# A decoder block's MLP, from one woven loop to two sweeps of seven products

## The chip, the cores and the metric

The kernel runs on one core of a Trainium2 chip. Its time is the device time of one execution in microseconds (us); lower is better. The five engines of a core are named as in the profile: PE multiplies matrices, DVE (VectorE) and ACT (ScalarE) work on tiles elementwise, POOL (GpSimd) and SP (SyncE) here mostly issue DMAs. PEld is PE's loading of the stationary operand, which overlaps its matmuls.

## The reference

One decoder layer on 512 tokens of width 2048, all float32. After a norm, an input projection, a delta-rule group, an attention group and an output projection, the part that the change touches is the MLP:

```python
h = h + jnp.einsum("bse,ed->bsd", mix, w_o[l])
u = rms_norm(h, mlp_norm[l])
hid = jnp.square(jax.nn.relu(jnp.einsum("bsd,df->bsf", u, w_up[l])))   # 2048 -> 8192
h = h + jnp.einsum("bsf,fd->bsd", hid, w_down[l])                      # 8192 -> 2048
return rms_norm(h, final_norm)
```

## The kernel before

**Products.** Every float32 operand is split into two float32r halves, `hi` (a rounding copy, on ACT, L147) and `lo` (the rest, a subtraction on DVE, L149). A product is then three matmuls: hi by hi, hi by lo, lo by hi. Weights come in as raw tiles of 512 KB ([128, 1024]) by DMAs of SP's queue, and `split`/`parts` makes `hi` and `lo` of each; there are 3 buffers for each of the two and 6 raw ones (`BUFS`).

**The MLP** starts at L947. `to_feature_major` scales `h`, turns it (transposes on PE, L185) and makes 16 pairs of halves `uT`, one for each 128 features. The hidden units are taken in 16 blocks of 512. `up_first` computes the first block's hidden units, 192 matmuls of 512 columns (L978 to 980). For each later block, `up_steps` computes four chunks of 128 hidden units by `cols_steps` (L204 to 206): the stationary operand is a 128x128 piece of `w_up`, the moving one all 512 tokens, so 16 feature blocks by 3 matmuls for a chunk, 192 for a block. The squared relu is L965 and L966.

**Down** goes by seven products. The block's hidden units (512 tokens by 512 units) are cut into four quarters a11 to a22 and the piece of `w_down` (512 by 1024, for each of two passes p) into four quarters b11 to b22. `seven_steps` makes seven factors of the hidden units, each split by `two` into halves that stay in SBUF (L800, L801). `block_steps` forms four sums of weight quarters on DVE (L864, 870, 878, 884) and runs seven products of 12 matmuls with 512 columns (L835 to 837), so 84 for a pass and 168 for a block, where the plain way would need 192. After most products its PSUM banks are added to `h` in SBUF, 16 additions of 128x512 a pass (L850, 852).

**Order.** The code's order is each engine's order. The loop at L996 weaves: while block b goes down, one step of the down products stands between pieces of the up product of blocks b+1 and b+2, and of the factors of block b+1. Block 15 goes down without the seven products (L1020 to 1036), woven with the end of block 14, and the final norm and the stores of the output follow by token tiles. SP issues a raw tile's load as soon as one of the 6 buffers is free.

Of the kernel before, what the change touches and what calls it, by code (L numbers as in the profile page):

```python
# [12 lines left out]
F32 = mybir.dt.float32  # L13
F32R = mybir.dt.float32r
AF = mybir.ActivationFunctionType
# [16 lines left out]
def hybrid_block(ctx: ExitStack, tc: tile.TileContext, x, attn_norm, w_in, conv_w, a_log, dt_bias,  # L32
# [758 lines left out]
    weave(chain(attn_values(1, dv[1]), attn_cols(2, df[2]), attn_cols(3, df[3])), att)  # L791


    def half_tile():

        return big("p", [P, 2, 2, 256], nm="hf")

    def two(src):
        z = big("w", [P, 2, 2, 256], F32R, nm="op")
# [4 lines left out]
    def seven_steps(left, f):  # L804

        a11, a21, a12, a22 = left[0][:, 0], left[0][:, 1], left[1][:, 0], left[1][:, 1]
        f["a12"] = two(a12)
        yield
        f["a11"] = two(a11)
        z = big("m", [P, 2, 2, 256], nm="s12")  # L810
        s1, s2 = z[:, 0], z[:, 1]
        V.tensor_add(s1, a21, a22)
        yield
        f["s1"] = two(s1)
        V.tensor_sub(s2, s1, a11)
        yield
        f["s2"] = two(s2)
        s4 = s1
        V.tensor_sub(s4, a12, s2)
        yield  # L820
        f["s4"] = two(s4)
        s3 = s2
        V.tensor_sub(s3, a11, a21)
        yield
        f["s3"] = two(s3)
        yield
        f["a22"] = two(a22)
        yield

    def product(bank, fac, wts, first, last_):  # L830
        (ah, al), (bh, bl) = fac, wts
        for k in range(2):
            for t in range(2):
                st = slice(t * P, (t + 1) * P)
                T.matmul(bank[t], lhsT=ah[:, k, st], rhs=bh[:, k, :], start=first and k == 0, stop=False, skip_group_check=True)  # L835
                T.matmul(bank[t], lhsT=ah[:, k, st], rhs=bl[:, k, :], start=False, stop=False, skip_group_check=True)  # L836
                T.matmul(bank[t], lhsT=al[:, k, st], rhs=bh[:, k, :], start=False, stop=last_ and k == 1, skip_group_check=True)  # L837

    def block_steps(f, w, row0, rows):

        for p in range(2):
            def quarter(i, j):
                r0, c0 = row0 + 256 * i, 1024 * j + 512 * p
                return load_w(w[r0:r0 + 256, c0:c0 + 512].rearrange("(k p) n -> p k n", p=P), [P, 2, 512])

            def add(bank, half, cg, op=ALU.add):
                for t in range(2):
                    dst = rows[2 * half + t][cg]
                    if op == ALU.add:
                        V.tensor_add(dst, bank[t], dst)  # L850
                    else:
                        V.tensor_sub(dst, dst, bank[t])

            b21, b11, b12, b22 = quarter(1, 0), quarter(0, 0), quarter(0, 1), quarter(1, 1)
            Y = [bank(), bank()]
            product(Y, f["a12"], parts(b21, 2), True, True)
            add(Y, 0, p)
            yield
            X = [acc(), acc()]
            product(X, f["a11"], parts(b11, 2), True, False)  # L860
            add(X, 0, p)
            yield
            t1 = b11
            V.tensor_sub(t1, b12, b11)  # L864
            Z = [acc(), acc()]
            product(Z, f["s1"], parts(t1, 2), True, False)
            add(Z, 1, p + 2)
            yield
            t2 = t1
            V.tensor_sub(t2, b22, t1)  # L870
            product(X, f["s2"], parts(t2, 2), False, False)
            add(X, 0, p + 2)
            yield
            product(Z, f["s4"], parts(b22, 2), False, True)
            add(Z, 0, p + 2)
            yield
            t3 = b12
            V.tensor_sub(t3, b22, b12)
            product(X, f["s3"], parts(t3, 2), False, True)
            add(X, 1, p)  # L880
            add(X, 1, p + 2)
            yield
            t4 = b21
            V.tensor_sub(t4, t2, b21)
            Y = [bank(), bank()]
            product(Y, f["a22"], parts(t4, 2), True, True)
            add(Y, 1, p, ALU.subtract)
            yield


    mixT = {}
# [52 lines left out]
    run(rows_steps(po, w_o[0], 3 * 512, 512, mix, by_token=4, done=finish))  # L944


    def up_unit(u):  # L947
# [4 lines left out]
    uT = to_feature_major(h, rstd, g_mlp)  # L952
    NBLK = DFF // 512

    def up_steps(b, j, left):
        z = half_tile()
        for k in range(2):
            po = sps()
            yield from cols_steps(po, w_up[0], (4 * b + 2 * j + k) * P, uT, tag="x")
            squared_relu(z, k, po)  # L960
        left.append(z)

    def squared_relu(z, k, po):
        r = big("m", [P, 512], nm="relu")
        A.activation(r, po, AF.Relu)  # L965
        A.activation(z[:, :, k, :], r.rearrange("p (i s) -> p i s", i=2), AF.Square)  # L966

    def up_first():

        po = [acc() for _ in range(4)]  # L970
        for u in range(KD // 2):
            hi, lo = up_unit(u) if u else first
            for j in range(2):
                k = 2 * u + j
                ah, al = uT[k]
                for c in range(4):
                    st = slice(c * P, (c + 1) * P)
                    T.matmul(po[c], lhsT=hi[:, j, st], rhs=ah, start=k == 0, stop=False)  # L978
                    T.matmul(po[c], lhsT=hi[:, j, st], rhs=al, start=False, stop=False)
                    T.matmul(po[c], lhsT=lo[:, j, st], rhs=ah, start=False, stop=k == KD - 1)  # L980
        for j in range(2):
            z = half_tile()
            for k in range(2):
                squared_relu(z, k, po[2 * j + k])
            lefts[0].append(z)

    def up(b, j):
        return up_steps(b, j, lefts[b]) if b < NBLK else iter(())

    lefts = [[] for _ in range(NBLK)]  # L990
    facs = [{} for _ in range(NBLK)]
    up_first()
    floor.clear()
    run(seven_steps(lefts[0], facs[0]))
    run(up(1, 0))
    for b in range(NBLK - 2):  # L996
        down = block_steps(facs[b], w_down[0], 512 * b, h)
        for p in range(2):
            ups = up(b + 1, 1) if p == 0 else up(b + 2, 0)
            fac = seven_steps(lefts[b + 1], facs[b + 1]) if p == 1 else iter(())  # L1000
            for i in range(7):
                next(down)
                next(fac, None)
                if i % 2 == 0:
                    next(ups, None)
            run(ups)


    down = block_steps(facs[NBLK - 2], w_down[0], 512 * (NBLK - 2), h)
    ups = up(NBLK - 1, 1)  # L1010
    for i in range(7):
        next(down)
        if i % 2 == 0:
            next(ups, None)
    run(ups)
    lft = lefts[NBLK - 1]
    fac = [[two(lft[j][:, i]) for i in range(2)] for j in range(2)]
    wts = {}

    def plain_steps(t):  # L1020
        for cg in range(4):
            po = bank()
            for j in range(2):
                if (cg, j) not in wts:
                    r0 = 512 * (NBLK - 1) + 256 * j
                    wts[cg, j] = split(w_down[0, r0:r0 + 256, cg * 512:(cg + 1) * 512].rearrange("(k p) n -> p k n", p=P),
                                       [P, 2, 512], ("u", "u"))
# [83 lines left out]
```

## Time and profile before

| | before |
|---|---|
| median of 3 runs (lowest to highest) | 2282.8 us (2282.29 to 2284.34) |
| the profiled execution | 2282.81 us, of which the span is 2281.1 |
| PE busy | 2245.4 us, 98% of the span |
| DVE busy | 1523.3 us, 67% |
| ACT busy | 887.8 us, 39% |
| POOL busy | 55.5 us, 2% |
| moved by DMA | 249.67 MB, 109 GB/s over the span |

The profile is one execution. Its page gives busy times by engine, a picture of the span in 40 slices, the DMA queues, the chain of work that ended last, and the costliest groups of instructions. Matmuls are pipelined: a matmul's listed duration (389 ns for 512 columns) is longer than the distance from one to the next, so durations of matmuls can't be added; the distances of starts can. The same holds to a smaller degree for DVE and ACT. Line numbers are those of the kernel before unless the text says otherwise.

### The profile page before, as it was taken

What the parts mean: (1) busy time and instruction counts of PE and PEld (TensorE: products, weight loads), DVE (VectorE), ACT (ScalarE), POOL (GpSimd) and SP (SyncE); (2) the same over time, 40 slices, a digit from 0 to 9 for tenths busy, and PEclk for the clock granted to TensorE, in tenths of its full rate; (3) what the DMA queues carried; (4) which work ended last, traced back from release to release, by engine and by line L of the source; (5) the groups of instructions that cost most, each with busy time, mean ns of one, the idle gap of its engine ahead of it and who ended that gap; (6) DMA issues with size and microseconds to landing.
All of it is one profiled execution on the core that took longest, in us unless ns stands there. A gap on an engine that the chain in (4) does not pass through costs nothing.

```text
span 2281.1 us, 27449 instructions
## 1 busy us (share of the span) xinstructions
PE 2245.4 (98%) x10649; PEld 1864.8 (82%) x10649; DVE 1523.3 (67%) x2338; ACT 887.8 (39%) x1444; POOL 55.5 (2%) x85
## 2 busy tenths in 40 slices
PE   8999999999999999999999999999999999999998
PEld 7988777778888788788888888888888888888887
DVE  5467787863355623437787687777778778777776
ACT  5233434432344523433344343343334334434343
POOL 0000100100000000000000000000000000000000
PEclk9999999999999999999999999999999999999999
DMA  8433333433232434233333333232332333323332
GB/s 282 141 111 95 109 97 96 117 92 110 85 95 88 139 92 151 83 105 98 109 93 119 95 99 113 93 123 90 98 115 93 115 98 95 118 93 120 93 127 95
DMA packets 288570, 249.67 MB, mean 109 GB/s; under 512 B 17300, under 2 KB 229560, under 8 KB 288440
## 3 DMA queue, kind: packets, MB, share of 16 engines
q1 hardware_dynamic: 287952, 247.72, 35.3%
q8 instruction: 83, 1.36, 0.3%
q14 instruction: 47, 0.39, 0.1%
q10 hardware_dynamic: 488, 0.21, 0.0%
HBM read 236.86 MB, written 11.03 MB: 109 GB/s over the span
## 4 chain that ended last, share of the span: by engine, by line
PE 90%; DVE 7%; ACT 1%; issue 1%; DMA 1%; POOL 0%; SPq 0%; ACTq 0%; POOLq 0%; DVEq 0%
PE s L206 10%; PE s L204 10%; PE s L205 10%; PE acc L837 6%; PE acc L836 6%; PE acc L835 6%; PE acc L204 5%; PE acc L205 4%; PE acc L206 4%; PE acc L220 3%; PE acc L221 3%; PE acc L222 3%; PE s L837 2%; PE s L836 2%; PE s L835 2%; DVE X L520 2%
## 5 line engine op out<-in xcount | busy, mean ns | idle before, releaser
L149 DVE TENSOR_TENSOR lo<-raw,hi 128x1024 fp32r<-128x1024 f32 (+2 forms) x370 | 443.9, 1200 | 342.3 <-ACT hi L147 337.5
L147 ACT ACTIVATE hi<-raw 128x1024 fp32r<-128x1024 f32 (+2 forms) x370 | 384.5, 1040 | 674.5 <-PE acc L205 136.7
L204 PE MATMUL s<-u,hi 128*128 128x512 f32 x960 | 373.4, 389 | 0.0
L205 PE MATMUL s<-u,hi 128*128 128x512 f32 x960 | 373.4, 389 | 0.0
L206 PE MATMUL s<-u,lo 128*128 128x512 f32 x960 | 373.4, 389 | 0.0
L149 DVE TENSOR_TENSOR lo<-x,hi 128x1024 fp32r<-128x1024 f32 x120 | 146.7, 1223 | 181.0 <-ACT hi L147 181.0
L204 PE MATMUL acc<-u,hi 128*128 128x512 f32 x640 | 260.6, 407 | 0.8 <-DVE dvl L679 0.6
L205 PE MATMUL acc<-u,hi 128*128 128x512 f32 x640 | 251.6, 393 | 0.0
L206 PE MATMUL acc<-u,lo 128*128 128x512 f32 x640 | 250.7, 392 | 0.0
L147 ACT ACTIVATE hi<-x 128x1024 fp32r<-128x1024 f32 x120 | 127.5, 1062 | 315.0 <-PE s L205 226.2
L836 PE MATMUL acc<-lo,op 128*128 128x512 f32 x600 | 233.4, 389 | 0.0
L837 PE MATMUL acc<-hi,op 128*128 128x512 f32 x600 | 233.4, 389 | 0.0
L835 PE MATMUL acc<-hi,op 128*128 128x512 f32 x600 | 233.1, 389 | 0.0
L850 DVE TENSOR_TENSOR h<-acc,h 128x512 f32<-128x512 f32 x360 | 232.2, 685 | 0.6 <-PE acc L837 0.5
L205 PEld LDWEIGHTS s<-u,hi 128*128 128x128 f32 x960 | 180.2, 188 | 37.4
L206 PEld LDWEIGHTS s<-u,lo 128*128 128x128 f32 x960 | 180.2, 188 | 37.4
L204 PEld LDWEIGHTS s<-u,hi 128*128 128x128 f32 x960 | 180.2, 188 | 37.4
L220 PE MATMUL acc<-hi,u 128*128 128x512 f32 (+2 forms) x384 | 144.7, 379 | 7.6 <-ACT hi L147 5.9
L204 PEld LDWEIGHTS acc<-u,hi 128*128 128x128 f32 x640 | 120.7, 189 | 25.0 <-DVE dvl L679 1.0
L206 PEld LDWEIGHTS acc<-u,lo 128*128 128x128 f32 x640 | 120.4, 188 | 25.3
L221 PE MATMUL acc<-lo,u 128*128 128x512 f32 (+2 forms) x384 | 140.5, 366 | 0.2 <-DVE lo L149 0.2
L222 PE MATMUL acc<-hi,u 128*128 128x512 f32 (+2 forms) x384 | 140.6, 366 | 0.0
(266 smaller groups left out, 3228.2 us busy)
## 6 DMA issues: line engine op xcount, KB each, us to landing
raw<-in_w_down_dram SPq DMA_DIRECT2D x128, 512.0 KB, 5.6
x<-in_w_up_dram SPq DMA_DIRECT2D x120, 512.0 KB, 4.2
raw<-in_w_in_dram SPq DMA_DIRECT2D x96, 512.0 KB, 3.9
raw<-in_w_o_dram SPq DMA_DIRECT2D x32, 512.0 KB, 3.8
raw<-in_w_in_dram SPq DMA_DIRECT2D x16, 384.0 KB, 8.3
w<-in_xt_dram SPq DMA_DIRECT2D x8, 512.0 KB, 8.5
p<-in_x_dram SPq DMA_DIRECT2D x8, 512.0 KB, 10.0
raw<-in_x_dram SPq DMA_DIRECT2D x8, 512.0 KB, 3.6
```

The lines of the kernel that those rows point to most:

```text
L147: A.activation(hi, raw, AF.Copy)
L149: floor["lo"] = V.tensor_sub(lo, raw, hi.bitcast(F32))
L204: T.matmul(po, lhsT=hi[:, j, :], rhs=ah, start=k == 0, stop=False)
L205: T.matmul(po, lhsT=hi[:, j, :], rhs=al, start=False, stop=False)
L206: T.matmul(po, lhsT=lo[:, j, :], rhs=ah, start=False, stop=k == KD - 1)
L220: T.matmul(o, lhsT=ah[:, st], rhs=bh, start=k == 0, stop=False)
L221: T.matmul(o, lhsT=ah[:, st], rhs=bl, start=False, stop=False)
L222: T.matmul(o, lhsT=al[:, st], rhs=bh, start=False, stop=k == KD - 1)
L835: T.matmul(bank[t], lhsT=ah[:, k, st], rhs=bh[:, k, :], start=first and k == 0, stop=False, skip_group_check=True)
L836: T.matmul(bank[t], lhsT=ah[:, k, st], rhs=bl[:, k, :], start=False, stop=False, skip_group_check=True)
L837: T.matmul(bank[t], lhsT=al[:, k, st], rhs=bh[:, k, :], start=False, stop=last_ and k == 1, skip_group_check=True)
L850: V.tensor_add(dst, bank[t], dst)
```

## The change

**Two sweeps.** The up products of all blocks are done first, then all down products. In the up sweep, `h` is parked in DRAM (`hscr`, 16 stores issued by POOL) and read back in the first down passes (`rows_back`), because its room holds factors of the normed input.

**Up by seven products.** For blocks 1 to 15 the product of input (512 tokens by 2048) and weights (2048 by 512) is cut in quarters too: tokens in two halves of 256, features in two halves of 1024, hidden units in two halves of 256. `u_factors` makes the factors of the input once, behind the matmuls of `up_first` (they stay in SBUF); `up_product` runs one of the seven products: 8 feature blocks by 2 pieces of 128 hidden units by 3, that is 48 matmuls with the 256 tokens of a half as columns. A block has 336 of them. Between products, copies on ACT and four two-input operations on DVE combine the PSUM banks into the four quarters of the hidden units, each followed by the squared relu on ACT.

**Weight sums.** Three sums of each weight unit are done on DVE (`sums`, and the first line of `one` in `adds`). The fourth, b22 plus b12, is done by a DMA from POOL's queue which reads b12 again from DRAM and accumulates it into the raw tile (`add_in`): two of 512 KB in each up block, and in the down sweep one for each block and pass. The sums stand unit by unit between the splits (`beside`).

**Factors through DRAM.** `keep` stores each of a block's seven factors (512 KB, both halves) by a DMA of POOL's queue; the down sweep loads them back through SP (`recall`). Block 15 has four plain quarters instead (`four_steps`).

**Down in groups.** The down sweep goes over the groups [0], [1, 2, 3], [4, 5, 6], [7, 8, 9], [10, 11, 12], [13, 14], in two passes each, with the same 84 matmuls of 512 columns for each block and pass; the products of a group's blocks accumulate in the same PSUM banks, and the 16 additions to `h` come once for a group and pass. Block 15 stays as it was. There are 9 raw buffers instead of 6, and twice the scratch for POOL's DMA descriptors.

```diff
-    BUFS = {"p": 10, "x": 2, "w": 8, "m": 2, "u": 16, "raw": 6, "hi": 3, "lo": 3}
+    BUFS = {"p": 10, "x": 2, "w": 8, "m": 2, "u": 16, "raw": 9, "hi": 3, "lo": 3}
...
+    def pair_of(src, tag):
+
+        z = big(tag, [P, 2, 2, 256], F32R, nm="op")
         A.activation(z[:, 0], src, AF.Copy)
         V.tensor_sub(z[:, 1], src, z[:, 0].bitcast(F32))
-        return z[:, 0], z[:, 1]
+        return z
+
+    fscr = {}
+
+    def keep(b, name, src):
+
+        z = pair_of(src, "w")
+        fscr[b, name] = dp.tile([P, 1024], F32, name=f"f_{name}_{b}")
+        G.dma_start(out=fscr[b, name], in_=z.bitcast(F32).rearrange("p a k s -> p (a k s)"))
...
+    def recall(b, name):
+        z = big("w" if name in ("a12", "a22") else "u", [P, 2, 2, 256], F32R, nm="fac")
+        with tc.issue_after(last_load[0].ins):
+            last_load[0] = nc.sync.dma_start(out=z.bitcast(F32).rearrange("p a k s -> p (a k s)"), in_=fscr[b, name])
+        return z[:, 0], z[:, 1]
+
+    def add_in(raw, src, k):
+
+        G.dma_start(out=raw.rearrange("p (k n) -> p k n", k=k), in_=src.rearrange("(k p) n -> p k n", p=P), accum_op=ALU.add)
+
+    def sums(out, a, b):
+
+        return [lambda o=o, x1=x1, x2=x2: V.tensor_add(o, x1, x2) for o, x1, x2 in zip(out, a, b)]
+
+    def adds(raws, srcs, k, a, b):
+        def one(z, src, x1, x2):
+            V.tensor_add(x1, x1, x2)
+            add_in(z, src, k)
+
+        return [lambda z=z: one(*z) for z in zip(raws, srcs, a, b)]
...
+    def u_factors():
+        for q in range(4):
...
+            def put(n, src, tag):
+                o = big(tag, [P, 2, 2, 256], F32R, nm="u" + n)
+                A.activation(o[:, :, 0, :], src, AF.Copy)
+                V.tensor_sub(o[:, :, 1, :], src, o[:, :, 0, :].bitcast(F32))
...
+    def up_product(bank, name, wts, first, last_, beside=()):
+
+        for n, raw in enumerate(wts):
+            bh, bl = parts(raw, 4)
+            if beside:
+                beside[n]()
+            for j in range(4):
+                k = 4 * n + j
+                ah, al = fu[name][k][:, 0, :], fu[name][k][:, 1, :]
+                for c in range(2):
+                    dst, st = bank[:, c * 256:(c + 1) * 256], slice(c * P, (c + 1) * P)
+                    head, tail = first and k == 0 and c == 0, last_ and k == 7
+                    T.matmul(dst, lhsT=bh[:, j, st], rhs=ah, start=head, stop=False, skip_group_check=True)
...
+        t4 = quarter(1, 0)
+        b12 = quarter(0, 1)
+        Y = bank()
+        up_product(Y, "a12", t4, True, True, sums(t1, t1, b12))
+        V.tensor_add(c11, Y, x1)
+        squared_relu(c11)
+        yield
+        b22 = quarter(1, 1)
+        Z = bank()
+        up_product(Z, "s1", t1, True, False, sums(t1, t1, b22))
+        A.activation(p5, Z, AF.Copy)
+        yield
+        up_product(X, "s2", t1, False, False)
+        A.activation(u2, X, AF.Copy)
+        yield
+        up_product(Z, "s4", b22, False, True, adds(b22, srcs(0, 1), 4, t4, t1))
+        V.tensor_add(c12, Z, u2)
+        squared_relu(c12, -1.0)
+        yield
+        Y = bank()
+        up_product(Y, "a22", t4, True, True)
+        A.activation(d4, Y, AF.Copy)
+        yield
+        up_product(X, "s3", b22, False, True)
...
+    left = up_first()
+    for b in range(1, NBLK):
+        fac, nxt = seven_steps(b - 1, left), []
+        for _ in up_steps(b, nxt):
+            next(fac, None)
+        run(fac)
+        left = nxt
+    last_fac = four_steps(NBLK - 1, left)
...
+    groups = [[0]] + [[b, b + 1, b + 2] for b in range(1, NBLK - 3, 3)] + [[NBLK - 3, NBLK - 2]]
+    for g in groups:
+        f = {}
         for p in range(2):
...
+            down = block_steps(g, f, p, w_down[0], h)
+            if g is groups[0]:
+                rows_back((p, p + 2))
+            if g is groups[-1] and p == 1:
+                break
+            for _ in down:
+                next(last_fac, None)
```

What moves is to be seen on three engines. PE, an up block: before, the end of a piece of an up product and the beginning of the next down product (`u` are the halves of the input, `op` factors of hidden units):

```order
L204 MATMUL s_10403<-u_8082,hi_10478 128x512
L205 MATMUL s_10403<-u_8082,hi_10478 128x512
L206 MATMUL s_10403<-u_8082,lo_10479 128x512
L835 MATMUL s_10517<-hi_10519,op_9957 128x512
L836 MATMUL s_10517<-lo_10520,op_9957 128x512
L837 MATMUL s_10517<-hi_10519,op_9957 128x512
L835 MATMUL s_10518<-hi_10519,op_9957 128x512
L836 MATMUL s_10518<-lo_10520,op_9957 128x512
L837 MATMUL s_10518<-hi_10519,op_9957 128x512
```

After, the beginning of block 1's first up product (`uh` are halves of the input's quarters, the same `hi` and `lo` tiles hold four feature blocks by 256 units):

```order
L1107 MATMUL acc_8465<-uh_7952,hi_8466 128x256
L1108 MATMUL acc_8465<-uh_7952,hi_8466 128x256
L1109 MATMUL acc_8465<-uh_7952,lo_8467 128x256
L1107 MATMUL acc_8465<-uh_7962,hi_8466 128x256
L1108 MATMUL acc_8465<-uh_7962,hi_8466 128x256
L1109 MATMUL acc_8465<-uh_7962,lo_8467 128x256
```

The moving operand has half the columns, the stationary pieces are of the same size, and no down product stands between the pieces.

POOL in the MLP. Before, its queue has the small powers of the MLP's norm and then those of the final norm:

```order
L128 TENSOR_TENSOR rstd_1266_7860<-rs_1267_7861,mhalf_82 128x1
L128 TENSOR_TENSOR rstd_1270_7881<-rs_1271_7882,mhalf_82 128x1
L128 TENSOR_TENSOR rstd_1274_7902<-rs_1275_7903,mhalf_82 128x1
L128 TENSOR_TENSOR rstd_1278_7923<-rs_1279_7924,mhalf_82 128x1
L128 TENSOR_TENSOR rstd_2807_17213<-rs_2808_17214,mhalf_82 128x1
L128 TENSOR_TENSOR rstd_2816_17253<-rs_2817_17254,mhalf_82 128x1
L128 TENSOR_TENSOR rstd_2828_17335<-rs_2829_17336,mhalf_82 128x1
L128 TENSOR_TENSOR rstd_2840_17417<-rs_2841_17418,mhalf_82 128x1
```

After, it has the stores of `h` between the powers of the norm, and in each up block seven stores of factors (`f_...`) and the two accumulating DMAs (L855), here block 2's with the factors of block 1:

```order
L812 DMA f_a11_1_9007<-op_1442_9004 128x1024
L812 DMA f_a12_1_9082<-op_1452_9079 128x1024
L812 DMA f_s1_1_9152<-op_1460_9149 128x1024
L855 DMA raw_1453_9085<-in_w_up_dram 128x4x256
L855 DMA raw_1454_9087<-in_w_up_dram 128x4x256
L812 DMA f_s2_1_9215<-op_1465_9212 128x1024
L812 DMA f_s4_1_9284<-op_1470_9281 128x1024
L812 DMA f_a22_1_9347<-op_1476_9344 128x1024
L812 DMA f_s3_1_9415<-op_1481_9412 128x1024
```

An accumulating DMA stands behind the stores of three factors and ahead of those of four others, in a queue that had no DMA.

DVE in the down products. Before, part of a pass of block 1, with the split of the next up block's weights (`x`) between products:

```order
L149 TENSOR_TENSOR lo_8625<-raw_8494,hi_8624 128x1024
L850 TENSOR_TENSOR h_7635<-acc_8573,h_7635 128x512
L850 TENSOR_TENSOR h_7639<-acc_8574,h_7639 128x512
L149 TENSOR_TENSOR lo_8643<-raw_8498,hi_8642 128x1024
L149 TENSOR_TENSOR lo_8667<-x_8664,hi_8666 128x1024
L850 TENSOR_TENSOR h_7627<-acc_8552,h_7627 128x512
L850 TENSOR_TENSOR h_7631<-acc_8553,h_7631 128x512
L149 TENSOR_TENSOR lo_8696<-raw_8496,hi_8695 128x1024
L850 TENSOR_TENSOR h_7627<-acc_8573,h_7627 128x512
L850 TENSOR_TENSOR h_7631<-acc_8574,h_7631 128x512
```

After, in the second pass of the group [0], whose only block is 0:

```order
L149 TENSOR_TENSOR lo_15884<-x_15877,hi_15883 128x1024
L859 TENSOR_TENSOR raw_15855<-raw_15855,raw_15879 128x1024
L899 TENSOR_TENSOR hb_15659<-s_15881,hb_15659 128x512
L149 TENSOR_TENSOR lo_15907<-raw_15855,hi_15906 128x1024
L899 TENSOR_TENSOR hb_15659<-s_15882,hb_15659 128x512
L859 TENSOR_TENSOR raw_15855<-raw_15855,raw_15902 128x1024
L899 TENSOR_TENSOR hb_15664<-s_15904,hb_15664 128x512
L863 TENSOR_TENSOR x_15877<-x_15877,raw_15855 128x1024
L899 TENSOR_TENSOR hb_15664<-s_15905,hb_15664 128x512
L149 TENSOR_TENSOR lo_15926<-raw_15855,hi_15925 128x1024
L149 TENSOR_TENSOR lo_15944<-raw_15902,hi_15943 128x1024
L149 TENSOR_TENSOR lo_15966<-x_15877,hi_15965 128x1024
```

The up block's splits and the factors are gone from between the products, so the additions to `h` (`hb` now) and the weight sums stand directly between the splits of one product and the next.

## Rows read from the trace of the kernel before

**Rows 1.** The page, part 1: busy time, share of the span, instructions of each engine.

```profile
PE 2245.4 (98%) x10649; PEld 1864.8 (82%) x10649; DVE 1523.3 (67%) x2338; ACT 887.8 (39%) x1444; POOL 55.5 (2%) x85
```

**Rows 2.** The page, part 4: the chain that ended last, by engine.

```profile
PE 90%; DVE 7%; ACT 1%; issue 1%; DMA 1%; POOL 0%; SPq 0%; ACTq 0%; POOLq 0%; DVEq 0%
```

**Rows 3.** Waits of PE: us in total, times, longest.

```profile
PE acc L220 <- ACT hi L147: 5.9, 2, 4.5
...
PE acc L978 <- ACT u L163: 0.3, 1, 0.3
```

**Rows 4.** Busy time in stretches: loads at the start, `up_first`, the woven loop.

```profile
core 0: us, PE busy (x) PEld busy (x) DVE busy (x) ACT busy (x) POOL busy (x), PEclk, DMA share, GB/s
10.00:40.00 30.00, 28.46 (x153) 27.82 (x154) 24.27 (x53) 21.23 (x38) 3.03 (x4) 1.00 1.05 389
955.60:1004.90 49.30, 49.24 (x240) 40.70 (x241) 21.67 (x25) 22.57 (x34) 0.00 (x0) 1.00 0.19 51
1100.00:1600.00 500.00, 500.00 (x2207) 414.01 (x2207) 376.83 (x448) 194.82 (x228) 0.00 (x0) 1.00 0.33 103
```

**Rows 5.** Timeline of PE, 256 columns: first and last of 9; start, us.

```profile
803.13 0.28 PE L733 MATMUL s<-dvh,at 128*128 128x256 f32 x1
...
804.08 0.28 PE L735 MATMUL s<-dvh,at 128*128 128x256 f32 x1
```

**Rows 6.** Timeline of PE, 272 columns: first and last of 55.

```profile
84.01 0.29 PE L220 MATMUL acc<-hi,u 128*128 128x272 f32 x1
...
90.83 0.29 PE L220 MATMUL acc<-hi,u 128*128 128x272 f32 x1
```

**Rows 7.** Timeline of PE's weight loads in the stretch of rows 5.

```profile
803.13 0.19 PEld L734 LDWEIGHTS s<-dvl,at 128*128 128x128 f32 x1
803.25 0.19 PEld L735 LDWEIGHTS s<-dvh,at 128*128 128x128 f32 x1
```

**Rows 8.** Groups by line, 1100 to 2100 us: busy, mean ns, idle before.

```profile
L149 DVE TENSOR_TENSOR lo<-raw,hi 128x1024 fp32r<-128x1024 f32 x172 | 210.3, 1223 | 106.8 <-ACT hi L147 106.8
L850 DVE TENSOR_TENSOR h<-acc,h 128x512 f32<-128x512 f32 x294 | 189.4, 685 | 0.0
...
L147 ACT ACTIVATE hi<-raw 128x1024 fp32r<-128x1024 f32 x172 | 181.8, 1057 | 283.6 <-PE s L205 103.8 <-PE acc L837 96.4 <-DVE raw L864 60.8
...
L864 DVE TENSOR_TENSOR raw<-raw,raw 128x1024 f32<-128x1024 f32 x25 | 30.5, 1219 | 0.0
...
L801 DVE TENSOR_TENSOR op<-hf,op 128x512 fp32r<-128x512 f32 x37 | 24.3, 684 | 0.0
L800 ACT ACTIVATE op<-hf 128x512 fp32r<-128x512 f32 x37 | 23.4, 633 | 25.8 <-PE acc L837 24.5
```

**Rows 9.** The chain by time at the MLP's norm: start, us, what.

```profile
950.96 0.70 DVE h L916
...
952.99 0.69 POOL rstd L128
...
953.70 1.34 ACT un L177 x2
955.04 0.58 ACT u L163
...
955.66 1.21 PE acc L978 x4
```

**Rows 10.** The page, part 6: DMA issues, KB each, us to landing.

```profile
raw<-in_w_down_dram SPq DMA_DIRECT2D x128, 512.0 KB, 5.6
x<-in_w_up_dram SPq DMA_DIRECT2D x120, 512.0 KB, 4.2
...
w<-in_xt_dram SPq DMA_DIRECT2D x8, 512.0 KB, 8.5
p<-in_x_dram SPq DMA_DIRECT2D x8, 512.0 KB, 10.0
...
yscr<-ut SPq DMA_DIRECT2D x4, 512.0 KB, 4.2
```

More of the change, by code (lines that the diff above doesn't have):

```diff
@@ L822, in seven_steps @@
-        s3 = s2
-        V.tensor_sub(s3, a11, a21)
+        keep(b, "s2", s2)
         yield
-        f["s3"] = two(s3)
+        negated_less(s1, s2, a12)
+        keep(b, "s4", s1)
         yield
-        f["a22"] = two(a22)
+        keep(b, "a22", a22)
+        V.tensor_add(s2, a11, a21)
         yield
-    def product(bank, fac, wts, first, last_):
-        (ah, al), (bh, bl) = fac, wts
-        for k in range(2):
-            for t in range(2):
[L834 to L888, printed above, removed]
@@ new lines, in seven_steps, with four_steps @@
+        keep(b, "s3", s2)
+        yield
+    def four_steps(b, left):
+        for j in range(2):
+            for i in range(2):
+                keep(b, f"a{i + 1}{j + 1}", left[j][:, i])
+                yield
[4 more added lines that the diff above has]
+        return z[:, 0], z[:, 1]
@@ new lines, in add_in, with product @@
+    def add_in(raw, src, k):
[7 more added lines that the diff above has]
+        return [lambda z=z: one(*z) for z in zip(raws, srcs, a, b)]
+    def product(bank, facs, wts, first, last_, beside=()):
+        for n, ((ah, al), raw) in enumerate(zip(facs, wts)):
+            bh, bl = parts(raw, 2)
+            if beside:
+                beside[n]()
+            for k in range(2):
+                for t in range(2):
+                    st = slice(t * P, (t + 1) * P)
+                    head, tail = first and n == 0 and k == 0, last_ and n == len(facs) - 1 and k == 1
+                    T.matmul(bank[t], lhsT=ah[:, k, st], rhs=bh[:, k, :], start=head, stop=False, skip_group_check=True)
+                    T.matmul(bank[t], lhsT=ah[:, k, st], rhs=bl[:, k, :], start=False, stop=False, skip_group_check=True)
+                    T.matmul(bank[t], lhsT=al[:, k, st], rhs=bh[:, k, :], start=False, stop=tail, skip_group_check=True)
@@ L980, in up_first @@
                     T.matmul(po[c], lhsT=lo[:, j, st], rhs=ah, start=False, stop=k == KD - 1)
+        floor.clear()
+        run(u_factors())
+        left = []
         for j in range(2):
@@ L983, in up_first @@
             for k in range(2):
[L984 to L997, printed above, removed]
-        for p in range(2):
[L999 to L1006, printed above, removed]
@@ L1009, in hybrid_block @@
[L1009 to L1017, printed above, removed]
+                r = big("m", [P, 512], nm="relu")
+                A.activation(r, po[2 * j + k], AF.Relu)
+                A.activation(z[:, :, k, :], r.rearrange("p (i s) -> p i s", i=2), AF.Square)
@@ new lines, in hybrid_block, with rows_back @@
+    left = up_first()
[6 more added lines that the diff above has]
+    last_fac = four_steps(NBLK - 1, left)
+    hb = []
+    for i in range(8):
+        z = big("p", [P, 2, 512], nm="hb")
+        hb.append(z)
+    h = [[hb[2 * cg + t // 2][:, t % 2, :] for cg in range(4)] for t in range(NT)]
+    def rows_back(cgs):
+        for cg in cgs:
+            for i in range(2):
+                with tc.issue_after(last_load[0].ins):
+                    last_load[0] = nc.sync.dma_start(out=hb[2 * cg + i], in_=hscr[2 * cg + i])
@@ L1024, in plain_steps @@
                 if (cg, j) not in wts:
+                    if not fac:
+                        fac.extend([[recall(NBLK - 1, f"a{i + 1}{j + 1}") for i in range(2)] for j in range(2)])
                     r0 = 512 * (NBLK - 1) + 256 * j
                     wts[cg, j] = split(w_down[0, r0:r0 + 256, cg * 512:(cg + 1) * 512].rearrange("(k p) n -> p k n", p=P),
[L1027 removed]
+                                       [P, 2, 512], ("x", "x") if cg == 3 and j else ("u", "u"))
                 bh, bl = wts[cg, j]
```

176 lines of the change are left out of this document (146 added, 30 removed).

## The prediction

> **What bounds the kernel now.** I read the page's first part, then the chain, then PE's waits, then the MLP by stretches. PE is busy 98% of the span, DVE 67% [rows 1]; the chain that ended last is PE for 90% [rows 2]; PE's longest wait for one partner sums to 5.9 us, and the matmuls of `up_first` waited 0.3 us [rows 3]. In the woven loop PE has no gap: 500.00 us busy of 500, at a granted clock of 1.00, which is the level of 2.4 GHz, while DVE has 377 us, ACT 195 and DMA a third of its share [rows 4]. So only fewer or shorter matmuls can shorten the MLP, and the rest has slack that the change may spend: DVE 123 us in 500, DMA two thirds. A 512-column matmul takes 500 / 2207 = 0.2266 us there, not its listed duration.
>
> **PE in the up products.** A block had 192 matmuls of 512 columns, 192 x 0.2266 = 43.5 us. It gets 7 x 48 = 336 of 256 columns. The trace has such matmuls in one place: eight distances from 803.13 to 804.08, 0.119 us each [rows 5]. The 272-column ones, 54 distances from 84.01 to 90.83, are at 0.126 [rows 6]. Half the columns thus cost 0.119 / 0.2266 = 0.525 of the time. I take 0.119: 336 x 0.119 = 40.0 us, 3.5 us less a block, and for 15 blocks -52.6 us. The stretch is read to 0.01 us at each end, 0.1175 to 0.120 for a distance, so the bounds are -60 and -48. The weight load of 128x128 lasts 0.19 us but starts every 0.12 us there [rows 7], so it overlaps and sets no limit at this spacing. The down products keep their 15 x 168 matmuls of 512 columns and `up_first` and block 15 theirs: nothing.
>
> The Trainium skill (TensorE: Matmul & The Clock Gate, Back-to-back issue gap) gives 262 cycles for 256 columns and 518 for 512. At 2.4 GHz that would be 0.109 and 0.216 us, a block's 41.4 to 36.7 us, and -71 us in the whole. Here the rows are above both figures, by 0.010 us for either size, and a fixed part of that kind is paid 336 times instead of 192; the measured spacing decides.
>
> **DVE in the up sweep.** A block needs 14 splits of 1.223 us, six weight sums of 1.22 (the seventh and eighth, the fourth sum of each unit, went to DMA), and 15 two-input operations of 0.685 (seven halves of factors, four factor sums, four combinations of products) [rows 8]: 17.1 + 7.3 + 10.3 = 34.7 us beside PE's 40.0. ACT has 14 copies of 1.057, seven of 0.633 and eleven more of about that length, some 26 us. Both fit, DVE at 87%, but in order: a combination (`c11`, `c12`, `c22`) waits for its product's last matmul and the next split stands behind it. With three buffers for halves, DVE runs at most about one and a half units ahead of PE. Placed by hand, unit by unit of 2.86 us, the tightest slack is 0.5 to 0.9 us, at the first split of the second product on sum t2, behind `c11`. I take +3 us for the sweep (0 to 8).
>
> **The fourth sum.** Before, it cost DVE 1.22 us [rows 8]. Now a DMA from POOL's queue adds 512 KB into the raw tile. It may be issued when s4's product has been split from that tile, and ACT's copy of the tile for s3's product waits for it, behind that DVE's split, and then PE. From the one to the other it is four units (two of s4's product, two of a22's), 4 x 2.86 = 11.4 us, and by my placing 1 to 2.4 us of lead of the splits over PE: 12.4 to 13.8 us in an up block. In the down sweep a unit is 12 x 0.2266 = 2.72 us: six units and some 2 us give 18 in groups of three, four give 13 in the pair, two give 7 in the group [0]. The trace of before has no such DMA and none on this queue. The nearest rows are plain 512 KB transfers: 4.2 and 5.6 us in the loop, 4.2 for a store, 8.5 and 10.0 at the start, where the queues are full at 389 GB/s [rows 4, 10]. I take up to 10 us, that is, hidden in all but the group [0] (price there below). At the low end it is as hidden, and no gain. At the high end, twice the 10.0 us, since the tile itself has to be read too, 20 - 13 = 7 us a block or 105 us in the sweep.
>
> The Trainium skill (DMA: Bandwidth & Descriptors, Anatomy of one DMA) fits transfers of this queue as 2.0 us plus bytes over 436 GB/s, 3.2 us for 512 KB, an estimate that leaves the sum as it is; it says nothing of an accumulating one, and no row shows any.
>
> **Stores and recalls of factors.** Seven stores of 512 KB stand in POOL's queue in each up block, one every 40 / 7 = 5.7 us. Of the eight `w` tiles four to six hold hidden units and products, so a split of a factor waits for the store two or three earlier, 11 us or more, against 4.2 us of a store [rows 10]. A late accumulation would hold up the stores queued behind it. Traffic in an up block is eight loads, two accumulations and seven stores of 512 KB, 8.9 MB in 40 us or 223 GB/s; a group of three has 24 loads, six accumulations and 21 recalls, 26.7 MB in 114 us or 234 GB/s, and 330 in its first pass if all recalls fell there. The start shows 389 [rows 4]. No term.
>
> **The start of the up sweep.** ACT gets 16 more copies of 512 columns (the plain input for its factors, 0.63 us each by the copies of [rows 8]) and the halves of the factors; DVE's four factor sums a quarter come too. ACT had 22.6 us in the 49.3 us of `up_first` [rows 4] and now has about 54 from the norm to the first up block, against PE's 50. Also POOL's powers of the norm, on the chain [rows 9], stand behind DMA issues of `h`'s stores. A power ahead of time is hidden; the last one is on the chain. I take +5 us (0 to 10).
>
> **The group [0].** One block and pass: seven splits, three sums and 16 additions to `h` on DVE, 8.6 + 3.7 + 11.0 = 23.2 us [rows 8], beside 84 x 0.2266 = 19.0 us of PE. Before, an up block's 43.5 us of PE stood beside each block; now nothing does. Two passes cost at least 2 x 4.2 = 8 us. The additions wait for products and the next splits stand behind them, so part of DVE's time can't overlap: placed by hand, 58 us instead of 38. I take +18 (8 to 25), which also holds the accumulation that is late here. In groups of three the additions come once: 21 x 1.22 + 9 x 1.22 + 11.0 = 47.6 us against 57.1 of PE, in the pair 35 against 38: no term. In all 480 additions become 192, 197 us less for DVE, off the path.
>
> **Sum.** 2282.8 of the profiled execution (the median is the same) - 52.6 + 3 + 18 + 5 = **2256 us**. The tail (end of the pair, block 15, final norm) keeps its order: 0, within 3.
>
> **Rivals.**
> (a) The accumulating DMA is late: it lands 17 us from its issue instead of under 13. PE then waits 4 us in each of 15 up blocks and each pass of the pair: 60 + 8, giving 2324. It decides from 1.7 us a block, a landing of 14.7 us, where the 26.6 us of gain are gone. For it: two sources, a queue shared with stores, a thin window; against it: plain loads at 4.2 to 5.6 us and a DMA share of a third [rows 4, 10].
> (b) The stage changes are hidden: raw tiles loaded early (9 buffers) and ACT ahead at the norm, group [0] at its DVE floor of 8. 2282.8 - 52.6 + 8 = 2238.
> (c) A 256-column matmul costs exactly half of a 512-column one in a long stream: 336 x 0.1133 = 38.1, -81.6 us, and with the other terms 2227. The Trainium skill's gap rule above (TensorE: Matmul & The Clock Gate) points this way. The measured spacings [rows 5, 6] speak against it.
> (d) The weight load limits: 336 x 0.19 = 63.8 us a block, +305 us, with the other terms about 2610. The loads that start every 0.12 us [rows 7] nearly exclude it.
> (e) DVE gets stuck behind stores of factors or behind combinations by 1.5 to 2 us a block, eating the gain: about 2282.
>
> **How the numbers follow.** Forecast 0.53, (a) 0.22, (b) 0.12, (c) 0.04, (d) 0.01, (e) 0.08. A measurement of this kernel tells about 0.2%, 4.6 us, from no change. Forecast, (b) and (c) are faster, 0.69; with a little of (e) 0.70. The rest of (e) is 0.06 within 0.2% and 0.01 slower, which with (a) and (d) makes 0.24. By the bounds of its terms the forecast alone reaches from 2231 to 2278. The low end of the range, 2232, takes in (b); (c) is left out below it. The high end, 2322, takes in (e) and the milder half of (a): a little under 2 in 10 is left out.
>
> **What would show it.** In the up sweep PE without gaps and 336 matmuls in 40 us: step one right; 38 or 37 would be (c). A wait of PE on a split behind `hi<-raw`, and that on a DMA of POOL's queue, of microseconds a block, would be (a), and the issue row of these DMAs gives the landing. In the group [0] PE should be busy about two thirds, waiting for DVE. PE should show a few us of idle between `up_first` and the first up block. The forecast is wrong if DVE exceeds 90% in the sweep, or if PE's spacing there differs from 0.119.

## The result and the profile after

The changed kernel takes **2300.1 us** (median of 4 runs, 2295.1 to 2302.4) where the kernel before takes 2282.6 beside it: a ratio of **1.0072** with a 95% interval of [1.0053, 1.0091], 17.5 us slower. 2256 was forecast. The profiled execution is of 2298.37 us with a span of 2296.4, 15.3 more than before.

The page's first part, as in [rows 1]:

```profile
PE 2223.9 (97%) x12809; PEld 1938.9 (84%) x12809; DVE 1580.7 (69%) x2296; ACT 1017.7 (44%) x1630; POOL 198.3 (9%) x270
```

PE is busy 21.5 us less and still ends later; its idle time went from 36 to 72 us. Where it is, the boundaries of the stages tell. The timeline of PE, start and duration in us: the first up product of block 1, the first matmul of the down sweep, the first of the group [1, 2, 3]. (Lines from here on are of the changed kernel, or of the experiment that is spoken of.)

```profile
1003.83 0.28 PE L1107 MATMUL acc<-uh,hi 128*128 128x256 f32 x1
...
1635.38 0.39 PE L877 MATMUL acc<-hi,fac 128*128 128x512 f32 x1
...
1699.73 0.40 PE L877 MATMUL acc<-hi,fac 128*128 128x512 f32 x1
```

Before, the first up product started at 1005.08. So:

| stretch | at PE's pace | before | after |
|---|---|---|---|
| ahead of the up products | | 1005.1 | 1003.8 |
| 15 up products | 652.6, now 604.8 | 652.6 | 631.6 |
| group [0] | 38.1 | 38.1 | 64.4 |
| other groups, block 15, tail | 576.5 | 585.3 | 596.6 |

The column "before" takes its woven products at the 0.2266 us of [rows 4], and the rest of the span as its tail: 8.8 us over PE's pace. PE's pace after takes the 5040 matmuls of 256 columns at 0.1200 us, their distance where nothing stops PE. The changed kernel has 26.8 us of loss in the up sweep, 26.3 in the group [0] and 20.1 behind it. That sums to 73.2 against 8.8 before: 64.4 of loss, less 47.8 of gain and 1.3 at the start, together the 15.3 of the spans.

Busy time in stretches (columns as in [rows 4]): the up sweep, the group [0], the groups of three.

```profile
core 0: us, PE busy (x) PEld busy (x) DVE busy (x) ACT busy (x) POOL busy (x), PEclk, DMA share, GB/s
1100.00:1300.00 200.00, 195.80 (x1611) 193.56 (x1610) 155.75 (x166) 116.48 (x158) 31.60 (x44) 1.00 0.76 221
1635.00:1700.00 65.00, 48.28 (x175) 34.52 (x174) 43.19 (x54) 18.28 (x22) 4.01 (x5) 0.89 0.80 286
1700.00:1900.00 200.00, 200.00 (x883) 165.36 (x882) 164.02 (x168) 78.52 (x74) 10.67 (x9) 1.00 0.72 238
```

The groups of three run without a gap. What PE waits for (us in total, times, longest) in the sweep, ...

```profile
PE acc L1109 <- DVE lo L149: 11.0, 23, 0.8
PE acc L1107 <- ACT hi L147: 0.7, 1, 0.7
```

... from the end of the sweep through the group [0], ...

```profile
PE acc L877 <- ACT hi L147: 10.2, 4, 5.2
PE s L878 <- DVE lo L149: 4.4, 4, 1.5
PE acc L1107 <- ACT hi L147: 4.1, 1, 4.1
```

... and in the last pass with block 15.

```profile
PE acc L878 <- DVE lo L149: 2.9, 1, 2.9
PE acc L877 <- ACT hi L147: 1.1, 1, 1.1
PE s L1216 <- ACT u L147: 1.1, 1, 1.1
```

PE waits for splits of weights everywhere, first copies on ACT, then subtractions on DVE. In the sweep it does so twice a block, 17.4 and 38.3 us from the block's start in nearly every one of the blocks 3 to 14. The chain behind the second of these, in block 6: the engine POOL with its two accumulating DMAs (in brackets the engine's idle time and what ended it), ...

```profile
1232.27 1.33 POOL L855 DMA_DIRECT2D raw<-in_w_up_dram  x1 [4.02 <-DVE lo L149]
1238.86 1.29 POOL L855 DMA_DIRECT2D raw<-in_w_up_dram  x1 [5.27 <-issue]
1239.64 1.08 POOL L812 DMA_DIRECT2D f_s<-op  x1
```

... and ACT, DVE and PE behind:

```profile
1246.94 1.06 ACT L147 ACTIVATE hi<-raw 128x1024 fp32r<-128x1024 f32 x1 [3.84 <-DMA raw<-in_w_up_dram]
1248.04 1.23 DVE L149 TENSOR_TENSOR lo<-raw,hi 128x1024 fp32r<-128x1024 f32 x1 [4.21 <-ACT hi L147]
1249.32 0.39 PE L1109 MATMUL acc<-uh,lo 128*128 128x256 f32 x1 [0.40 <-DVE lo L149]
```

The first accumulation is issued at 1232.27 and has landed at 1238.54 (6.28 us). The second, whose tile was split by 1233.6, is issued only at 1238.86, 0.3 us behind that landing, with idle time that nothing in the profile explains ("issue"). It lands at 1246.86, ACT's copy follows at 1246.94, DVE's split at 1248.04, and PE stops until 1249.3. In all 15 blocks the second accumulation starts 0.3 us behind the first's landing. In the groups of three, where rows of `w_down` are 2 KB long instead of 1 KB, three of them start 2.7 us apart while the one before is still on its way. The landing itself is not long, us from issue, smallest, median, largest of the sweep's 30:

```profile
DMA to landing us min/median/max: 5.8/7.2/11.1
```

So the late tile is not a slow DMA but one that is held ahead of its issue.

### The profile page after: what moved, and what is told of

It is laid out like the page before. It is cut to its first block, busy times and chain, and to the rows that moved or that the text cites. A ratio compares the mean times of both kernels' runs of the same rounds, so it can differ in the third digit from the quotient of the medians.

```text
span 2296.4 us, 32952 instructions
## 1 busy us (share of the span) xinstructions
PE 2223.9 (97%) x12809; PEld 1938.9 (84%) x12809; DVE 1580.7 (69%) x2296; ACT 1017.7 (44%) x1630; POOL 198.3 (9%) x270
## 5 line engine op out<-in xcount | busy, mean ns | idle before, releaser
L149 DVE TENSOR_TENSOR lo<-raw,hi 128x1024 fp32r<-128x1024 f32 (+2 forms) x520 | 624.9, 1206 | 418.6 <-ACT hi L147 408.7
L147 ACT ACTIVATE hi<-raw 128x1024 fp32r<-128x1024 f32 (+2 forms) x520 | 543.2, 1046 | 788.7 <-PE acc L205 134.6
L878 PE MATMUL s<-lo,fac 128*128 128x512 f32 x480 | 187.3, 390 | 4.4 <-DVE lo L149 4.4
L877 PE MATMUL s<-hi,fac 128*128 128x512 f32 x480 | 186.4, 390 | 0.6 <-DMA fac<-f_s 0.3
L879 PE MATMUL s<-hi,fac 128*128 128x512 f32 x480 | 186.9, 389 | 0.0
L877 PE MATMUL acc<-hi,fac 128*128 128x512 f32 x360 | 142.9, 398 | 11.3 <-ACT hi L147 11.3
L878 PE MATMUL acc<-lo,fac 128*128 128x512 f32 x360 | 143.6, 399 | 4.4 <-DVE lo L149 4.4
L859 DVE TENSOR_TENSOR raw<-raw,raw 128x1024 f32<-128x1024 f32 x120 | 146.1, 1219 | 2.1 <-DMA raw<-in_w_down_dram 0.5
L1109 PE MATMUL acc<-uh,lo 128*128 128x256 f32 x480 | 138.6, 289 | 5.4 <-DVE lo L149 5.4
L879 PE MATMUL acc<-hi,fac 128*128 128x512 f32 x360 | 142.8, 397 | 0.0
L1107 PE MATMUL acc<-uh,hi 128*128 128x256 f32 x480 | 137.5, 286 | 4.9 <-ACT hi L147 4.9
L205 PEld LDWEIGHTS acc<-u,hi 128*128 128x128 f32 x640 | 120.8, 189 | 23.8 <-issue 1.4
L1108 PE MATMUL acc<-uh,hi 128*128 128x256 f32 x480 | 137.0, 285 | 0.0
L1107 PE MATMUL s<-uh,hi 128*128 128x256 f32 x480 | 135.8, 283 | 0.0
## 6 DMA issues: line engine op xcount, KB each, us to landing
fac<-f_s SPq DMA_DIRECT2D x60, 512.0 KB, 10.4
```

The source lines that it names most:

```text
L147: A.activation(hi, raw, AF.Copy)
L149: floor["lo"] = V.tensor_sub(lo, raw, hi.bitcast(F32))
L205: T.matmul(po, lhsT=hi[:, j, :], rhs=al, start=False, stop=False)
L859: return [lambda o=o, x1=x1, x2=x2: V.tensor_add(o, x1, x2) for o, x1, x2 in zip(out, a, b)]
L1107: T.matmul(dst, lhsT=bh[:, j, st], rhs=ah, start=head, stop=False, skip_group_check=True)
```

## Experiments

### The queue's room

```diff
-"raw": 9
+"raw": 8
-dynamic_dma_scratch_size=2048
+dynamic_dma_scratch_size=4096
```

> The changed kernel with twice the scratch for the descriptors of POOL's DMAs (4096 instead of 2048), and 8 raw buffers instead of 9 to make room. Theory: in each up block the second accumulating DMA is issued only 0.3 us after the first has landed (6.6 us after the first's issue), because the queue has no room for the descriptors of two; so ScalarE's copy for the second unit of s3's product comes late and PE stops 0.6 us some 38 us into the block. With the room, the second is issued 1.3 to 1.6 us after the first, that stop is gone (9 us in the sweep), and so is the wait of 4 us at the sweep's end: 2300 becomes 2284 to 2291. Rival: the queue does one accumulation at a time whatever its room, or the stop has another cause: 2297 to 2303, the second still behind the first's landing.

Measured: **2267.7 us**, ratio 0.9936 [0.9921, 0.9951]. POOL's two accumulations of a block, and PE in a stretch of the sweep:

```profile
1184.97 1.31 POOL L855 DMA_DIRECT2D raw<-in_w_up_dram  x1 [3.84 <-DVE lo L149]
1187.92 1.30 POOL L855 DMA_DIRECT2D raw<-in_w_up_dram  x1 [1.64 <-DVE lo L149]
...
1100.00:1300.00 200.00, 200.00 (x1669) 200.00 (x1669) 163.91 (x174) 120.90 (x164) 31.42 (x44) 1.00 0.76 224
```

The second now starts 2.95 us behind the first, with only the split of its tile to wait for. PE has no idle time in the sweep, which takes 604.8 us, and every block takes 40.3. The gain, 32.4 us, is twice the upper end that was expected: not one of the two stops went, but both, and the wait at the sweep's end with them. The group [0] still takes 63.7.

That run had changed the raw buffers too, so they were changed alone (`"raw": 8`, scratch 2048):

> The changed kernel with 8 raw buffers instead of 9 and nothing else: the other half of what the run with more scratch had changed. Theory: that run's 32 us are the scratch's alone, so here the second accumulating DMA still starts 6 to 7 us after the first, the up sweep still takes about 631 us, and the time stays at 2296 to 2304. Rival: fewer loads in flight ahead are what freed the accumulations; then the sweep comes to 605 us and the time to 2270.

Measured: 2297.4 us, ratio 1.0062 [1.0047, 1.0077]; the sweep takes 634.3 us, with both stops, and the second accumulation is held as ever. It starts 0.3 us behind the landing of the first, at 1198.55; its own tile had been split by 1193.0, and the split that the row names is another, which happened to end just before:

```profile
1191.64 1.31 POOL L855 DMA_DIRECT2D raw<-in_w_up_dram  x1 [4.01 <-DVE lo L149]
1198.87 1.30 POOL L855 DMA_DIRECT2D raw<-in_w_up_dram  x1 [5.91 <-DVE lo L149]
```

Then the scratch alone, up by a quarter (2560) and down by a quarter (1536), with 9 raw buffers:

> The changed kernel with a scratch of 2560 instead of 2048 and all 9 raw buffers: the smallest step that leaves the rest alone. Theory: what holds the second accumulating DMA is room, and the first needs more than half of 2048; whether a quarter more is enough the traces don't tell. If it is, the second starts 2.7 to 3.1 us after the first, the sweep takes 605 us, and the time is 2266 to 2272, as with 4096. If the room of two is over 2560, nothing moves: 2296 to 2303, which bounds the need from below and leaves the theory standing. Rival, that any part of the 32 us came from another effect of the larger scratch: a time between, with the second's start still behind the first's landing.

> The changed kernel with a scratch of 1536 and all 9 raw buffers: less room. Theory: more of POOL's DMAs wait for one before them to land; the sweep gets longer than 631 us, and in groups of three the accumulations, which start 2.7 us apart with 2048, may start 6 us apart; 2305 to 2340. Rival: the scratch matters only above some size, and 1536 is as 2048: 2296 to 2303.

Measured: with 2560 **2269.1 us**, ratio 0.9938 [0.9923, 0.9953], sweep 604.8; with 1536 2299.2 us, ratio 1.0072 [1.0055, 1.0089], sweep 633.2. POOL in a block with 2560:

```profile
1183.96 1.33 POOL L855 DMA_DIRECT2D raw<-in_w_up_dram  x1 [4.21 <-DVE lo L149]
1186.79 1.29 POOL L855 DMA_DIRECT2D raw<-in_w_up_dram  x1 [1.50 <-DVE lo L149]
```

For the time it is a threshold between 2048 and 2560, not a slope: the second accumulation of 1 KB rows either finds room or waits for the first to land. Of the two expectations for 1536 the rival's time held: 1536 is no slower than 2048. Yet part of the theory came true there as well. In the groups of three, POOL with 1536 (first three lines) and with 2048 (last three):

```profile
1843.14 1.20 POOL L855 DMA_DIRECT2D raw<-in_w_down_dram  x1 [49.07 <-DVE lo L149]
1845.81 1.19 POOL L855 DMA_DIRECT2D raw<-in_w_down_dram  x1 [1.46 <-DVE lo L149]
1849.28 1.18 POOL L855 DMA_DIRECT2D raw<-in_w_down_dram  x1 [2.28 <-issue]
...
1844.38 1.19 POOL L855 DMA_DIRECT2D raw<-in_w_down_dram  x1 [50.54 <-DVE lo L149]
1847.05 1.18 POOL L855 DMA_DIRECT2D raw<-in_w_down_dram  x1 [1.47 <-DVE lo L149]
1849.77 1.18 POOL L855 DMA_DIRECT2D raw<-in_w_down_dram  x1 [1.54 <-DVE lo L149]
```

With 1536 the third of the three is held too: in each of the eight passes it starts 0.3 us behind the landing of the first (here at 1848.96), with idle time put down to "issue" or to another DMA. It costs nothing there, since PE waits nowhere in these groups. So 1536 has room for two accumulations of 2 KB rows and not for three, 2048 for three and not for two of 1 KB rows, 2560 for these two. A tile of 512 KB is 256 rows of 2 KB or 512 of 1 KB. If it is rows that take up the room, which no run tests by itself, then, as an estimate from these starts, 1536 has room for 512 to 767 rows, 2048 for 768 to 1023 and 2560 for 1024 or more.

### The order of the sums on DVE

```diff
-            V.tensor_add(x1, x1, x2)
+            with tc.issue_after(floor["lo"].ins):
+                V.tensor_add(x1, x1, x2)
```

> The changed kernel with the two VectorE sums for a22's product placed behind the split of the same unit of s4's product, instead of ahead of the splits of s2's product. Theory: PE's stop of 0.5 to 0.8 us some 17 us into each up block comes from these 2 x 1.22 us, which stand ahead of the first split of s2's product while VectorE works without a gap. Moved, 14 x 0.6 = 8 to 10 us less: 2288 to 2292. Rival, as in the prediction: the addition that makes c11, waiting for its product, holds the split; then nothing moves: 2297 to 2303.

Measured: 2287.8 us, ratio 1.0027 [1.0018, 1.0037]. The total is at the lower end of the theory's range, but not by its way. PE's waits in the sweep (us in total, times, longest; lines are one further down in this kernel):

```profile
PE acc L1110 <- DVE lo L149: 8.3, 13, 0.8
PE acc L1108 <- ACT hi L147: 3.4, 4, 0.9
```

The stop at 17 us is gone, as expected, but the one at 38 us has grown to between 0.3 and 1.9 us, and the sweep takes 629.8 us, 1.7 less. Most of the gain lies in the group [0] (58.3 instead of 64.4) and behind it (3.4 less); what the later sums do there was not followed up. So the stop at 17 us needs two things: the two sums ahead of the split, and a DVE that comes late out of the block before because it stood idle for the held accumulation (4.2 us at 1248.04). With more scratch the sums stand where they stood and there is no stop.

### The group [0]

```diff
-    groups = [[0]] + [[b, b + 1, b + 2] for b in range(1, NBLK - 3, 3)] + [[NBLK - 3, NBLK - 2]]
+    groups = [[0, 1], [2, 3, 4], [5, 6, 7], [8, 9, 10], [11, 12], [13, 14]]
```

> The changed kernel with other groups in the down sweep: [0,1], [2,3,4], [5,6,7], [8,9,10], [11,12], [13,14], so none of a single block. Theory: the group [0] took 66.2 us for 38.1 us of matmuls since VectorE has more to do than PE there and the accumulation (8.7 to 10.1 us from issue to landing) has only 7 us; a pair has 35.4 of VectorE beside 38.1 of PE and 13 us for it. Of the 28 us lost 20 to 26 come back: 2274 to 2280. Rival: the loss belongs to the change of sweep (recalls, h and weights together at the limit of the DMA engines), whatever the first group is: 2293 to 2303, with PE's waits on loads and recalls.

Measured: 2279.6 us, ratio 0.9985 [0.9976, 0.9994]. (The 66.2 us in the expectation are read with matmuls that the timeline had run together; counted one by one the group [0] took 64.4.) PE's waits in the first pair:

```profile
PE acc L878 <- DVE lo L149: 1.4, 2, 0.8
PE acc L877 <- ACT hi L147: 0.6, 1, 0.6
```

The pair is 2.9 us over its 76.1 of PE, where the single block was 26.3 over; the sweep is 6 us longer here (637.5), its last block 51.8 instead of 47.9, so not all of it shows in the total. The group's loss is its own, and the rival falls for this kernel.

### Without the accumulating DMAs

```diff
             V.tensor_add(x1, x1, x2)
-            add_in(z, src, k)
```

> The changed kernel without the accumulating DMAs: b22 plus b12 is left out, so s3's product gets b22 alone; 30 MB less are moved. Theory: the accumulations cost the stop at 38 us into each block (9 us), the wait at the sweep's end with the half clock after it (6), 5 us of wait and some half clock in each pass of the group [0] (14), and 4 to 6 at the end of the pair: 2262 to 2272. Rival: they are hidden and these waits have other causes: 2295 to 2303.

Measured: 2253.6 us, ratio 0.9874 [0.9859, 0.9888]. The sweep takes 604.8 us without any wait of PE, as with more scratch: the accumulations were all of its loss, and with room for them they cost it nothing. The time is below the theory's range, which had put only 15 of the sweep's 26.8 us down to them. The group [0] falls to 51.0 us, from 63.7 with more scratch. So its loss is about half accumulation (12.6 us, where it lands 10.1 and 7.6 us from its issue in the two passes of the run with more scratch). The other 13.0 us are there without it: PE waits 4.5 us for DVE's splits and 3.3 for ACT, and has slow matmuls behind these waits. That DVE, with more work there than PE, is the cause of this half is likely but not shown by a run of its own. Two of these waits (lines are one further up in this kernel):

```profile
PE s L877 <- DVE lo L149: 3.7, 3, 1.5
PE s L876 <- ACT op L802: 1.7, 1, 1.7
```

### Both together, and the tail

> Scratch of 4096, 8 raw buffers, and the groups [0,1], [2,3,4], [5,6,7], [8,9,10], [11,12], [13,14]. Theory: the two losses lie in different stretches and add up: the first group's loss falls from 25.6 us (with the scratch alone) to about 3, so 2267.7 - 22.6 = 2245 (2242 to 2249). Rival: with the sweep at its full pace, recalls and h's loads come later against it, and the pair waits for them: 2252 to 2262.

The edits are those of the queue's room and of the group [0] above. Measured: 2252.2 us, ratio 0.9867 [0.9853, 0.9882], above the theory's range and at the lower end of the rival's. The sweep is at 604.8, but the first pair loses 7.6 us instead of 2.9. PE waits 3.2 us in it for a recalled factor, where it waited for none in the run with pairs alone, so the rival has a part after all.

```diff
     for i in range(7):
         next(down)
-        next(steps[0 if i < 4 else 1], None)
```

> As the run with scratch and pairs, but block 15's plain products are not woven with the last pass: they all stand behind it. Theory: the last stretch has 8 us more than before the change, since the splits of block 15's weights stand between those of the pair in ScalarE's and VectorE's queues, where VectorE is already at nine tenths; behind the pass they have 43 us of PE to themselves: 5 to 8 us less, 2238 to 2241. Rival: the products behind it then wait for their own splits and the additions of the pair: no gain, or 3 us more.

Measured: **2241.8 us**, ratio 0.9820 [0.9804, 0.9837], 10.4 less than the run before it, where 5 to 8 less were expected, from a time of that run 7 us lower than it came out. From the last pass on, the span is 8.8 us over PE's pace instead of 17.7, and PE waits nowhere in it: as much as before the change. The first pair is what remains; DMA is full in it (PE 40.45 of 45 us, DMA share 1.04, 385 GB/s):

```profile
1609.00:1654.00 45.00, 40.45 (x169) 32.10 (x168) 32.64 (x38) 18.47 (x21) 4.00 (x5) 0.96 1.04 385
```

> As the run before it, and the sums for a22's product behind the splits of s4's product. Theory: the sweep already runs without a stop, so there is nothing to gain there; where VectorE is nearly full (the last pair) the earlier run gained 3 us with it. 0 to 3 us less than the run before. Rival: the stop at 17 us into a block had its own cause in these sums: then the run with more scratch would have kept it, which it did not.

The added edit is that of the sums on DVE above. Measured: **2240.8 us**, ratio 0.9818 [0.9803, 0.9832]. The difference to the run before, 1 us, is about its scatter. All of PE's waits of 0.5 us and more from 1600 us on:

```profile
PE s L878 <- DMA fac<-f_a: 3.5, 1, 3.5
PE acc L879 <- DVE lo L149: 0.6, 1, 0.6
```

> As the run with scratch, pairs, tail and late sums, but with a scratch of 2560 and all 9 raw buffers. Theory: the sweep and the groups of three are at PE's pace with either; what is left is the first pair, where DMA moves 385 GB/s and PE waits 3.5 us for a recalled factor. A ninth buffer lets SP load weights earlier, into a stretch that is full already, so it changes nothing: 2238 to 2243. Rival: with it the loads are out of the way before the recalls; the first pair loses 3 to 5 us less: 2234 to 2237.

Two numbers differ from the run before it, `"raw": 9` and 2560. Measured: 2240.7 us, ratio 0.9817 [0.9800, 0.9833]; the ninth buffer changes nothing, and the first pair still loses 6.7 us. These last two are the fastest, 1.8% under the kernel before.

## Why the prediction was wrong, point by point

**The fourth sum** is the step that failed. It took the accumulating DMA as hidden up to a landing of 10 us, in a window of 12.4 to 13.8 counted from the split of its tile, and the landings were 5.8 to 11.1 us, median 7.2: the size was right. What it took for granted is that the DMA is issued when its tile is split. The second of a block was issued 5.2 us later than that (block 6) and landed 13.2 us from its split, at the very edge of the window, which made stops of 0.3 to 1.0 us. The part on stores named POOL's queue and a wait for buffers of stores, and not that the queue itself has room for so much and no more. The section on the change names that room ("twice the scratch"), and the prediction has no term for it. Rival (a) had the right place and the right sign, by a wrong cause (a long landing) and with 4 us a block where it was about 1.8; its 2324 is 24 us above the result.

**The loss in the sweep** was put at 3 us, with 8 as the upper bound. It was 26.8, by the starts of the matmuls: some 16 us in 25 stops of the blocks, 5.4 in three at the end of the sweep, and 5.7 in 60 distances of some 0.21 us instead of 0.12. Of the 60, 31 stand singly, nearly each behind a stop, at a granted clock of 1.00. The other 29, 2.7 us in all, stand in two stretches at half the clock, in block 12 and at the sweep's end. Block 12 in three stretches (columns as in [rows 4]):

```profile
1490.00:1499.00 9.00, 9.00 (x77) 8.93 (x75) 3.21 (x4) 3.37 (x6) 2.27 (x4) 1.00 0.95 237
1499.00:1502.00 3.00, 1.50 (x8) 1.16 (x7) 1.89 (x3) 2.48 (x4) 0.00 (x0) 0.89 0.88 346
1502.00:1505.00 3.00, 3.00 (x16) 3.00 (x16) 2.96 (x3) 1.35 (x2) 0.53 (x1) 0.54 0.93 302
```

PE stood still for half of 1499 to 1502, and from there the clock is at its lower level of 1.2 GHz until some 1504.5, with the spacing that goes with it. Behind the single stops of the other blocks it stays at 1.00 (1003.8 to 1499, with 20 stops, has 1.00 on the mean). The prediction had no term for that; in the group [0], with its waits of 4 to 5 us, it is there again (0.89 on the mean). The tightest place was named right, the first split of s2's product behind `c11`, 17.4 us into a block, with a slack of 0.5 to 0.9; the runs show that the two sums ahead of it and the late DVE use it up, not `c11` alone. DVE's work was not put too low: it was busy 155.75 us of 200 in the sweep, 78% against the 87% of the prediction.

**PE's gain** was right in kind and 5 us too large. The distance of the 256-column matmuls is 0.1200 us in the undisturbed stretches, against 0.119 from eight distances [rows 5]; 336 of them make 40.3 us, 15 blocks 47.8 us less. The bounds were -60 and -48, so it came out just beyond the smaller one. Rivals (c) and (d) fall. By the Trainium skill's figure for isolated matmuls (TensorE: Matmul & The Clock Gate, Back-to-back issue gap) it would be 0.109; the trace has 0.011 more in a stream of 5040 matmuls, so what was read off nine holds to 0.001.

**The group [0]** was put at 18 us (8 to 25) and cost 26.3. Without accumulations it cost 13, with the same placing; the accumulation, which the term was to hold with the rest, is 12.6 alone: it lands after 10.1 and 8.7 us, where 5.9 is the median of the down sweep and the window was 7. At the first of the two, loads, recalls and `h` fill the DMA engines (1640 to 1665: DMA share 1.04, 388 GB/s).

**The start** was put at +5 and was -1.3: ACT had 48.1 us busy of the 60 from 950 on, and PE waited for it 0.7 us. **The tail** was put at 0 and cost 11: that its order is the same does not help, since the pair has two blocks' splits in a pass and block 15's stand between them. Without the weaving, in the kernel with more scratch and no single-block group, it is 0.

The sum of the corrections to the forecast: 4.8 for PE, 23.8 for the sweep, 8.3 for the group [0], 11.3 behind it, -6.3 at the start: 41.9, and 2256 + 42 = 2298, the profiled execution.

## What to carry to other kernels

A DMA that is late is late by its issue or by its flight; read both, the engine's row of the issue beside the landing, and where the issue waits for nothing that the profile names, look whether it follows the landing of another DMA of the same queue. Descriptor scratch for POOL's queue is a resource with a threshold; a quarter more of it was worth 31 us here, and the whole change turns from 0.7% slower to 1.8% faster with that, an unwoven tail and no single-block group. A stop can have a second cost, since the clock may fall behind it; in the sweep it did so in two places, and not behind the single stops of up to 1 us.

## What the runs showed that was not expected

The issue of an accumulating DMA with 1 KB rows holds POOL until the one before has landed with a scratch of 1536 or 2048, and does not with 2560 or 4096. With 2 KB rows the third of three is held with 1536, until the first has landed, and not with 2048. The accumulating DMA is about as slow as the stores issued around it: 512 KB landed after 5.7 to 11.1 us, median 6.3 over both sweeps, against a median of 6.9 for plain stores of the factors s1 to s4, many of which stand behind an accumulation. The quickest accumulation took about twice as long as the quickest store, 5.7 us against 2.9; the stores of the a factors have a median of 3.2.
